# The two branch gates as 2x2 by 2x2 block products of seven, three formed inside the recurrence and four after it

## The chip, the cores and the metric

The kernel runs on one core of one Trainium2 chip. The metric is the device time of one launch in microseconds (us); a comparison takes the median of several runs. All arithmetic that counts is float32, so a matrix product is made of three matmuls: each operand x is split into a rounded high part h (fp32r) and a low part l = x - h, and hh + hl + lh is accumulated in PSUM.

## The reference, cut to what matters

```python
xn = rmsnorm(x, norm1_g)                   # 1024 tokens x 1024 channels
u  = xn @ w_in                             # q,k,v | f,i,q,g of HGRN2 | gate_sb | gate_hg
o_sb = stick_breaking_attention(q_sb, k_sb, v_sb)
o_hg = rmsnorm(hgrn2(silu(q_hg), k_hg, i_hg, log_f)) * silu(g_hg)
g_a = sigmoid(gate_sb + bg[:1024]);  g_b = sigmoid(gate_hg + bg[1024:])
merged = g_a * (o_sb @ w_o_sb) + g_b * (o_hg @ w_o_hg)
h = x + merged @ w_out
h = h + square(relu(rmsnorm(h) @ w_ff1)) @ w_ff2
out = rmsnorm(h) * final_g
```

The change concerns the two gates: `gate_sb` and `gate_hg` are each xn (1024 x 1024) times 1024 columns of `w_in`, and the two products with `w_o_sb` and `w_o_hg` that they scale.

## The kernel before, in words

Channels lie on partitions, tokens on the free axis, in two halves of 512 tokens (`halves`). `xn` is kept as eight pairs of tiles (`Acts`: high and low part, for each half of the tokens and each 256 channels). A product of one block of 128 output channels with one half of the tokens is `proj_half` (L471): eight k-tiles of 128 channels, three matmuls of 128x512 each (`three`, L466), so 24 matmuls into one PSUM bank.

The stages are: norm and transposes, attention, recurrence of HGRN2, gates and output projections, `w_out` with the second norm, MLP up (`UpPair`) and MLP down. The MLP products are already made as 2x2 block products of seven.

The engines' order is written by the program. Work that fills TensorE is put in a `Stream` (L413): a list of jobs, each with weight units that are loaded and split one or two jobs ahead (`prefetch`), and a generator that yields every six matmuls. The recurrence of the four heads runs as "main" work: `hg_levels` makes per head one diagonal product (`sd`) and seven levels (`sl`), where VectorE scales k and q between two levels, and `hg_tail` carries the state across chunks (`pk`, `pkv`, `pho`, `pot`). Between two pieces of main work the driver at L1476 takes FILL steps (2.8 to 4) from the stream; `upto` says how far the stream may go in each head. A scheduling layer then orders each engine's queue by these priorities, allots the buffers (40 full slots of 128x1024, 10 half slots, two each of `raw`, `whi`, `wlo`, eight PSUM banks) and puts in the waits. Each engine and the DMA queue of SP work through their queue in order.

The gates are jobs of that stream: for each branch (`which`) and each of eight column blocks (`cb`) one `proj_jobs` with `gate_epilogue` (L958, ScalarE's sigmoid with bias), 48 matmuls of 128x512. After every two blocks comes `out_job` (L968): the output projection of that branch (12 matmuls for each block and half), multiplied by the gate on VectorE. Branch 0 runs as fill of the recurrence (`pjg00` to `pjg07`, `py00` to `py07`), branch 1 after it, then `merged_split` makes the split tiles `ms` that `w_out` reads.

In `hg_tail` the loops write one 128-column piece of a PSUM bank and have it read (VectorE at L885 and L887 for `pkv`, ScalarE's square at L908 for `pho`) before the next piece is written.

Of the kernel before, what the change touches and what calls it, by code (L numbers as in the profile page):

```python
# [9 lines left out]
F32 = mybir.dt.float32  # L10
# [9 lines left out]
P = 128  # L20
# [8 lines left out]
NHG = 4  # L29
# [10 lines left out]
def kernel(  # L40
# [79 lines left out]
    def matmul(*a, **k):  # L120
        return pe(nc.tensor.matmul(*a, **k))  # L121
# [740 lines left out]
    def hg_tail(h):  # L862
# [32 lines left out]
        yield  # L895
        ons = []
        for half in range(2):
            open_block("main")
            po = bank(f"pho{h}_{half}")
            ssq = small.tile([P, 4], F32, tag="ssq4", name=f"hss{h}_{half}")  # L900
            sq = small.tile([P, P], F32, tag="sq", name=f"hsq{h}_{half}", bufs=1)
            for j in range(4):
                c = 4 * half + j
                cs, js = slice(c * P, (c + 1) * P), slice(j * P, (j + 1) * P)
                matmul(po[:, js], sc[:, cs], v[:, cs], start=True, stop=c == 0)
                if c:
# [40 lines left out]
            return h[:, s], l[:, s]  # L947

    a_sb, a_hg = Split("asb"), Split("ahg")
    mg, gate = {}, {}  # L950
    mgs = Acts("ms")

    def merged_split(half, kp):
        hi, lo = mgs.make(half, kp)
        for j, cs in halves():
            hi_lo(hi[:, cs], lo[:, cs], mg[2 * kp + j][:, half * 512 : (half + 1) * 512])

    def gate_epilogue(which, cb):  # L958
        def ep(ps, half):
            if half == 0:  # L960
                gate[which, cb] = slot(f"g{which}{cb}")
            b = prm[:, BG + which * KT + cb : BG + which * KT + cb + 1]
            dst = gate[which, cb][:, half * 512 : (half + 1) * 512]
            nc.scalar.activation(dst, ps, AF.Sigmoid, bias=b)  # L964

        return ep

    def out_job(which, cp):  # L968
        mat = (W_OSB, W_OHG)[which]
        src = mat[:, cp * 256 : (cp + 1) * 256].rearrange("(k p) c -> p k c", p=P)  # L970
        unit = Unit(f"wo{which}{cp}", [[(0, 256, src)]])
        acts = (a_sb, a_hg)[which]

        def body():
            if which == 1 and cp == 3:
                for kp in range(3):
                    merged_split(1, kp)
            for half, cs in halves():
                for j in range(2):
                    cb = 2 * cp + j  # L980
                    ps = bank(f"py{which}{cb}_{half}")
                    yield from proj_half(
                        ps, unit.hl[0], acts.mov, 4, half, lambda k: k * 256 + j * P
                    )
                    g = gate[which, cb][:, cs]
                    if which == 0:
                        if half == 0:
                            mg[cb] = slot(f"mg{cb}")
                        mul(mg[cb][:, cs], ps, g)
                    else:  # L990
                        mul(g, ps, g)
                        nc.vector.tensor_tensor(
                            out=mg[cb][:, cs], in0=mg[cb][:, cs], in1=g, op=ALU.add
                        )
                if which == 1 and (half == 0 or cp == 3):
                    merged_split(half, cp)
                    if cp == 3:
                        st.prefetch()

        return st.add([unit], body)  # L1000

    j_out = {}
    for which in range(2):
        for cp in range(4):
            for cb in (2 * cp, 2 * cp + 1):
                c0 = (C_GA, C_GB)[which] + cb * P
                u = cols_unit(f"wg{which}{cb}", [(W_IN, c0, P)])
                proj_jobs([(f"pjg{which}{cb}", u, gate_epilogue(which, cb))], xn)
            j_out[which, cp] = out_job(which, cp)


    hres = []
    scratch = ctx.enter_context(
        tc.tile_pool(name="scratch", bufs=1, space=bass.MemoryType.DRAM)
    )

    def dram(name, shape):
        return scratch.tile(shape, F32, tag=name, name=name)

    hn = Quads()  # L1020
    hsrc, hd = {}, {}
# [13 lines left out]
    def wout_job(n):  # L1035
        cs = slice(n * 512, (n + 1) * 512)
        units = [
            Unit(
                f"wout{n}{i}",
                [[(0, 512, W_OUT[i * 256 : (i + 1) * 256, cs].rearrange("(k p) c -> p k c", p=P))]],  # L1040
                wide=True,
            )
            for i in range(4)
        ]

        def body():
            for tb in range(NT):
                if n == 0:
                    hres.append(slot(f"h{tb}"))
                    load(hres[tb], X[tb * P : (tb + 1) * P, :])  # L1050
                    if tb in AHEAD_AT:
                        st.prefetch()
# [10 lines left out]
        return st.add(units, body)  # L1063

    AHEAD_AT = (2, 4, 6)
    for n in range(2):
# [4 lines left out]
    NPAIR, NCH = FF // 256, FF // 512  # L1071
    ad = [dram(f"ad{c}", [P, 7, 2, 512]) for c in range(NCH)]

    def half(name, dt=F32):
        return hpool.tile([P, 512], dt, tag="h", name=name)
# [5 lines left out]
    def add(out, a, b):  # L1081
        nc.vector.tensor_tensor(out=out, in0=a, in1=b, op=ALU.add)

    def sub(out, a, b):
        nc.vector.tensor_tensor(out=out, in0=a, in1=b, op=ALU.subtract)

    class UpPair:
        def __init__(self, j):
# [384 lines left out]
    st.finish(j_hg[0])  # L1473


    FILL = (2.8, 2.8, 2.8, 3, 4)  # L1476
    owed = 0.0
    turns = 0
    for h in range(NHG + 1):
        lev = hg_levels(h) if h < NHG else iter(())  # L1480
        tail = hg_tail(h - 1) if h > 0 else iter(())
        upto = (j_hg[2], j_hg[3], j_hg[3] + 2, j_out[0, 1], j_out[0, 3])[h]
        going = True
        while going:
            going = False
            if h == NHG - 2:
                p = len(a_sb.t)
                turns += 1
                if turns > 3 and p < 4:
                    a_sb.put(p, osb[p])  # L1490
# [15 lines left out]
    st.finish(j_wout - 2)  # L1506
    st.advance(7, j_wout - 1)
    first[0].load()
    first[0].split()
    first[0].sums()  # L1510
    st.finish(j_wout - 1)
    first[1].load()
    g2b[0] = slot("g2b")
    load(g2b[0], norm2_g[0].partition_broadcast(P))
    for tb in range(NT):
        st.advance(1, j_wout)
        if tb == 1:
            first[1].split()
            first[1].sums()
# [11 lines left out]
            pass  # L1531
        if tb == 6:
            hn.sums(1, 1)
    st.finish(j_wout)
    pairs[2].load()
    first[1].w1(0, 256)
    first[0].w2(0, 256)
# [65 lines left out]
```

## Time and profile before

| | |
|---|---|
| median of 3 runs | 1518.85 us (1517.78 to 1519.51) |
| the profiled execution | 1516.4 us, of which the span of instructions is 1514.6 us |
| granted TensorE clock | 0.999 |
| busy: PE, VectorE (DVE), ScalarE (ACT), GpSimd (POOL) | 1483.2, 962.1, 616.2, 69.1 us |
| DMA | 172.21 MB, mean 114 GB/s |

Stages in the span: norm and attention to about 329 us, recurrence with its fill to about 632 us, the rest of the gates and output projections to 795 us, `w_out` and second norm to about 900 us, then the MLP. PE counts matmuls, PEld weight loads. A matmul's end is modelled, so the distance between starts tells more than its duration. "L121" is the helper `matmul`; the tiles tell the products apart: `pjg` gates and HGRN2's g, `py` output projections, `sd` and `sl` the recurrence's levels, `pk`, `pkv`, `pho`, `pot` its tail. In the chain that ended last each row has its start, its length, the engine, the tile and the number of instructions.

### The profile page before, as it was taken

Reading aid. Unit: us, or ns where it says so; the run is one execution under the profiler, and the core shown is the slowest. Engines: PE = TensorE matmul, PEld = TensorE weight load, DVE = VectorE, ACT = ScalarE, POOL = GpSimd, SP = SyncE. Lnnn points to the kernel's source line nnn. Section 1 sums busy time; section 2 is a strip of 40 time slices with the busy share of each in tenths; the row PEclk is TensorE's granted clock in tenths of the full one; section 3 lists DMA queues with packets and bytes.
Section 4 is the critical chain, followed back from the end, with each engine's and each line's share of the span. In section 5 each row is a group of like instructions: output and inputs, shape, how many; then the busy total and the mean of one; then the engine's idle time right before and its main releaser. Section 6 shows DMA issues by size and latency. Waiting matters only on the chain.

```text
span 1514.6 us, 19739 instructions
## 1 busy us (share of the span) xinstructions
PE 1483.2 (98%) x7677; PEld 1258.7 (83%) x7677; DVE 962.1 (64%) x1379; ACT 616.2 (41%) x1091; POOL 69.1 (5%) x242
## 2 busy tenths in 40 slices
PE   7999999999999999999999999999999999999997
PEld 6888988988898888888888888888888878888886
DVE  5689798786535554232344479766666857757765
ACT  6566566541312211222232275444444434443433
POOL 2011010000000000000000000000000000000020
PEclk9999999999999999999999999999999999999999
DMA  7123012001101011111115232344444996654744
GB/s 202 29 56 77 8 53 67 15 15 43 57 1 42 29 38 33 42 56 42 56 56 195 111 107 96 127 153 152 153 153 153 341 374 250 222 202 172 260 141 170
DMA packets 125716, 172.21 MB, mean 114 GB/s; under 512 B 22924, under 2 KB 76216, under 8 KB 125624
## 3 DMA queue, kind: packets, MB, share of 16 engines
q1 hardware_dynamic: 124088, 166.77, 32.2%
q0 software_dynamic: 1536, 4.20, 1.2%
q8 instruction: 60, 0.98, 0.3%
q14 instruction: 32, 0.26, 0.0%
HBM read 129.00 MB, written 37.75 MB: 110 GB/s over the span
## 4 chain that ended last, share of the span: by engine, by line
PE 77%; DVE 5%; issue 5%; ACT 2%; DMA 2%; POOL 1%; SPq 0%; POOLq 0%; DVEq 0%; ACTq 0%
PE pm L121 15%; PE pjg L121 14%; PE pX L121 8%; PE py L121 6%; PE pY L121 5%; PE pW L121 5%; PE pw L121 4%; PE sl L121 3%; PE pjf L121 3%; PE pji L121 3%; PE pjq L121 2%; PE po L121 2%; PE pjv L121 1%; DVE rm L646 1%; PE z L121 1%
## 5 line engine op out<-in xcount | busy, mean ns | idle before, releaser
L134 ACT CAST whid<-w 128x1024 fp32r<-128x1024 f32 x31 | 32.7, 1055 | 166.7 <-PE pm L121 114.9
L646 DVE TENSOR_TENSOR_SCAN rm<-rm,bits 128x895 f32<-128x895 f32 (+5 forms) x64 | 86.1, 1349 | 18.8 <-ACT rm L627 17.1
L121 PE MATMUL pm<-whid,sl 128*128 128x512 f32 x248 | 96.6, 389 | 0.7 <-DVE sl L137 0.7
L121 PE MATMUL pm<-whid,sh 128*128 128x512 f32 x248 | 96.6, 390 | 0.6 <-ACT sh L134 0.6
L121 PE MATMUL pm<-wlod,sh 128*128 128x512 f32 x248 | 96.5, 389 | 0.0
L121 PE MATMUL pm<-th,sl 128*128 128x512 f32 x200 | 77.9, 390 | 0.4 <-DVE sl L137 0.4
L121 PE MATMUL pm<-tl,sh 128*128 128x512 f32 x200 | 77.8, 389 | 0.0
L121 PE MATMUL pm<-th,sh 128*128 128x512 f32 x200 | 77.8, 389 | 0.0
L137 DVE TENSOR_TENSOR sl<-sa,sh 128x1024 fp32r<-128x1024 f32 x56 | 68.3, 1220 | 2.0 <-ACT sh L134 2.0
L137 DVE TENSOR_TENSOR wlod<-w,whid 128x1024 fp32r<-128x1024 f32 x31 | 37.9, 1224 | 39.9 <-ACT whid L134 39.6
L134 ACT CAST wTh<-pw 128x128 fp32r<-128x128 f32 (+3 forms) x96 | 44.0, 484 | 45.9 <-PE pw L124 42.8
L134 ACT CAST sh<-sa 128x1024 fp32r<-128x1024 f32 x56 | 57.9, 1049 | 3.4 <-DMA sa<-ad 3.2
L121 PEld LDWEIGHTS pm<-whid,sl 128*128 128x128 f32 x248 | 46.5, 188 | 10.8 <-DVE sl L137 1.2
L121 PEld LDWEIGHTS pm<-whid,sh 128*128 128x128 f32 x248 | 46.6, 188 | 10.7 <-ACT sh L134 1.0
L137 DVE TENSOR_TENSOR wTl<-pw,wTh 128x512 fp32r<-128x512 f32 (+3 forms) x96 | 50.5, 547 | 7.6 <-ACT wTh L134 4.5
L121 PEld LDWEIGHTS pm<-wlod,sh 128*128 128x128 f32 x248 | 46.5, 188 | 9.6
L121 PEld LDWEIGHTS sl<-q,k 128*128 128x128 f32 (+1 forms) x448 | 50.2, 184 | 2.9 <-issue 1.1
L144 DVE TENSOR_TENSOR bt<-bt,rm 128x895 f32<-128x895 f32 (+5 forms) x64 | 48.2, 755 | 5.0 <-ACT bt L630 0.3
L121 PE MATMUL sl<-q,k 128*128 128x128 f32 (+1 forms) x448 | 51.3, 268 | 0.0
L964 ACT ACTIVATE g<-pjg,prm 128x512 f32<-128x512 f32 x32 | 21.9, 686 | 71.7 <-PE pjg L121 71.7
L121 PE MATMUL pX<-sqh,t1l 128*128 128x512 f32 x128 | 49.9, 390 | 0.5 <-DVE t1l L137 0.5
L627 ACT ACTIVATE rm<-z 128x511 f32<-128x511 f32 (+6 forms) x96 | 47.3, 500 | 7.6 <-DVE bt L144 4.5
(798 smaller groups left out, 4398.6 us busy)
## 6 DMA issues: line engine op xcount, KB each, us to landing
w<-in_w_ff_dram SPq DMA_DIRECT2D x72, 512.0 KB, 4.5
sa<-ad SPq DMA_DIRECT2D x56, 512.0 KB, 6.9
ad<-a SPq DMA_DIRECT2D x32, 256.0 KB, 3.8
ad<-s SPq DMA_DIRECT2D x16, 512.0 KB, 3.3
x<-in_x_dram SPq DMA_DIRECT2D x8, 512.0 KB, 4.5
h<-in_x_dram SPq DMA_DIRECT2D x8, 512.0 KB, 8.0
hd<-h SPq DMA_DIRECT2D x8, 512.0 KB, 2.7
ad<-p SPq DMA_DIRECT2D x16, 256.0 KB, 4.5
```

The source lines that it names most:

```text
L121: return pe(nc.tensor.matmul(*a, **k))
L134: after(nc.scalar.copy(dst, src), hold[0])
L137: return nc.vector.tensor_tensor(out=dst, in0=src, in1=hi.bitcast(F32), op=ALU.subtract)
L144: nc.vector.tensor_tensor(out=out, in0=a, in1=b, op=ALU.mult)
L627: nc.scalar.activation(rm[:, s0 + c0 - 1 : s0 + m - 1], z[:, c0:m], AF.Sigmoid, scale=-0.125)
L646: nc.vector.tensor_tensor_scan(out=rr, data0=rr, data1=bits[:, 1024 - nk : 1023][:, ::-1], initial=0.0, op0=ALU.mult, op1=ALU.max,)
L964: nc.scalar.activation(dst, ps, AF.Sigmoid, bias=b)
```

## The change

Both gates are taken together as one block product. The token halves are rows 1 and 2 of a 2x2 matrix A (A11, A12, A21, A22: half of the tokens by half of the channels of xn), and the columns of branch a and branch b are the columns of a 2x2 matrix B. For each of the eight column blocks seven products (of 12 matmuls of 128x512) replace eight.

- Three on the plain xn: A11 B11, then A22 times a difference of weights, then A12 B21 (`raw_job`, 36 matmuls). They run as fill of heads 2 and 3. Their results go to DRAM (`pd`, and the finished gate of branch a for the first half, `gd`).
- The output projection of branch a (`sb_job`) comes behind them as fill; it reads `gd` back and writes its products to DRAM (`yd`). Beside it `sum_forms` makes four sums of A's blocks: eight DMAs of 512 KB on POOL's queue that add the high tile onto the low tile in SBUF, then adds, subtractions and splits on VectorE and ScalarE.
- The other four products and the output projection of branch b run after the recurrence (`gates`): per block X6, Y5, X7, the late half's projection, Y3, the early half's projection, 72 matmuls. The next block's weights are loaded, differenced and split meanwhile (`GatePair.split`), `pd` and `yd` are loaded back, and three quarters of the late half's merged rows go through DRAM (`md`).
- In `hg_tail` the pieces of `pkv` and of `pho` are all written before the first is read.
- FILL is 3 throughout, `upto` follows the new jobs, and `w_out` has a stream of its own that splits ahead from its first job.

```diff
-        def __init__(self):
+        def __init__(self, eager=False):
...
-            if self.pos > 0:
+            if self.pos > 0 or self.eager:
                 self.prefetch()
...
                 matmul(pkv[:, js], ktk[:, cs], v[:, cs], start=True, stop=True)
+            for j in range(4 - half):
+                c = 4 * half + j
+                cs, js = slice(c * P, (c + 1) * P), slice(j * P, (j + 1) * P)
                 dst = Ss[:, (c + 1) * P : (c + 2) * P]
...
                     matmul(po[:, js], qh[:, cs], Ss[:, cs], start=False, stop=True)
+            for j in range(4):
+                js = slice(j * P, (j + 1) * P)
                 nc.scalar.activation(sq, po[:, js], AF.Square, accum_out=ssq[:, j : j + 1])
...
+    class RawUnit(Unit):
...
+            hi_lo(h, l, ra)
+            sub(rb, ra, rb)
+            sub(rb[:, 512:], rb[:, 512:], rb[:, 0:512])
+            self.hl = [(h, l)]
...
+    def raw_job(cb):
...
+        def body():
+            p1, p14, g1 = (half(f"{n}_{cb}") for n in ("p1", "p14", "g1"))
+            ps, p4 = bank(f"pga{cb}"), bank(f"pgq{cb}")
+            yield from steps_of(ps, 0, 0, 0, 0, True)
+            nc.scalar.copy(p1, ps)
+            nc.sync.dma_start(pd[cb][:, 0, :], p1)
+            for v in raw_units[cb : cb + 2]:
+                v.split_t()
+            yield from steps_of(p4, 1, 0, 1, 4, True)
+            add(p14, p1, p4)
+            nc.sync.dma_start(pd[cb][:, 1, :], p14)
+            yield from steps_of(ps, 0, 4, 0, 4, False)
+            nc.scalar.activation(g1, ps, AF.Sigmoid, bias=gate_bias(0, cb))
+            nc.sync.dma_start(gd[cb], g1)
+            if cb >= 4:
+                a_sb.put(cb - 4, osb[cb - 4])
...
+    def sum_forms():
...
+        def whole(i, j, kp):
+            h, l = (t.bitcast(F32) for t in xn.t[i, 2 * j + kp])
+            nc.gpsimd.dma_start(l, h, accum_op=ALU.add)
+            raw[i, j, kp] = l
...
+        for i, j in ((1, 0), (1, 1), (0, 0), (0, 1)):
+            for kp in range(2):
+                whole(i, j, kp)
+        yield from range(4)
...
+            add(s1[kp], raw[1, 0, kp], raw[1, 1, kp])
+            sub(s2[kp], s1[kp], raw[0, 0, kp])
+            split(6, kp, s2[kp])
...
+    class GatePair:
...
+        def x7(self):
+            self.product(7, self.X, False)
+            p1, p14 = self.p[:, 0:512], self.p[:, 512:1024]
+            add(p1, p1, self.X)
+            add(p1, p1, self.Y)
+            add(p14, p14, self.X)
+            self.gate(p1, 1)
+            self.gate(p14, 0)
...
+    def gates():
+        for cb in range(KT):
+            v = gp[cb]
+            n = gp[cb + 1] if cb + 1 < KT else None
+            v.x6()
+            v.y5()
+            if n:
+                n.split()
+                n.load_sums()
+                if cb + 2 < KT:
+                    gp[cb + 2].load()
+            else:
+                wout_units[0][0].split()
+            v.x7()
+            v.late_half()
+            v.y3()
+            v.early_half()
...
-    FILL = (2.8, 2.8, 2.8, 3, 4)
+    FILL = (3, 3, 3, 3, 3)
...
-        upto = (j_hg[2], j_hg[3], j_hg[3] + 2, j_out[0, 1], j_out[0, 3])[h]
+        upto = (j_hg[2], j_hg[3], j_raw[5], j_sb[1], j_sb[3])[h]
...
-    st.finish(j_out[0, 3])
-    for h in range(NHG):
-        a_hg.put(h, ohg[h])
-    st.finish(j_out[1, 3])
+        if h > 1:
+            a_hg.put(h - 2, ohg[h - 2])
+    a_hg.put(NHG - 1, ohg[NHG - 1])
+    st.finish(j_sb[3])
+    gates()
```

More of the change, by code (lines that the diff above doesn't have):

```diff
@@ L949 @@
     a_sb, a_hg = Split("asb"), Split("ahg")
-    mg, gate = {}, {}
     mgs = Acts("ms")
[L953 to L1012, printed above, removed]
     scratch = ctx.enter_context(
@@ L1018, in dram, with half, add, sub @@
         return scratch.tile(shape, F32, tag=name, name=name)
+    def half(name, dt=F32):
+        return hpool.tile([P, 512], dt, tag="h", name=name)
+    def add(out, a, b):
+        nc.vector.tensor_tensor(out=out, in0=a, in1=b, op=ALU.add)
+    def sub(out, a, b):
+        nc.vector.tensor_tensor(out=out, in0=a, in1=b, op=ALU.subtract)
+    pd = [dram(f"pd{cb}", [P, 2, 512]) for cb in range(KT)]
+    gd = [dram(f"gd{cb}", [P, 512]) for cb in range(KT)]
+    yd = [dram(f"yd{cb}", [P, 2, 512]) for cb in range(KT)]
@@ new lines, with gate_bias, gate_cols, __init__ @@
+    md = [dram(f"md{kp}", [P, 2, 512]) for kp in range(KT // 2)]
+    def gate_bias(which, cb):
+        return prm[:, BG + which * KT + cb : BG + which * KT + cb + 1]
+    def gate_cols(which, cb):
+        c0 = (C_GA, C_GB)[which] + cb * P
+        return slice(c0, c0 + P)
+    class RawUnit(Unit):
+        def __init__(self, cb):
+            dmas = [
+                [(0, P, W_IN[:, gate_cols(w, cb)].rearrange("(k p) c -> p k c", p=P))]
+                for w in range(2)
+            ]
+            super().__init__(f"wga{cb}", dmas)
+        def split(self):
+            if self.hl is not None:
+                return
+            self.load()
+            ra, rb = self.raw
+            h, l = (
+                wpool.tile([P, 1024], F32R, tag=t, name=f"{self.name}{t}") for t in ("whi", "wlo")
+            )
+            hi_lo(h, l, ra)
+            sub(rb, ra, rb)
+            sub(rb[:, 512:], rb[:, 512:], rb[:, 0:512])
+            self.hl = [(h, l)]
+        def split_t(self):
+            if len(self.hl) == 1:
+                t = slot(f"{self.name}t", F32R)
+                self.hl.append((t[:, 0:512], t[:, 512:]))
+                hi_lo(*self.hl[1], self.raw[1][:, 512:])
@@ new lines, with steps_of @@
+    raw_units = [RawUnit(cb) for cb in range(KT)]
+    def raw_job(cb):
+        u = raw_units[cb]
+        def steps_of(ps, wt, w0, half_, k0, start):
+            wh, wl = u.hl[wt]
+            for k in range(4):
+                c = (w0 + k) * P
+                xh, xl = xn.mov(k0 + k, half_)
+                three(
+                    ps, wh[:, c : c + P], wl[:, c : c + P], xh, xl, start and k == 0, k == 3, True
+                )
+                if k % 2 == 1:
+                    yield
+        def body():
[14 more added lines that the diff above has]
+                a_sb.put(cb - 4, osb[cb - 4])
+        return st.add([u], body)
@@ new lines, with sb_job, body @@
+    side = []
+    def sb_job(cp):
+        src = W_OSB[:, cp * 256 : (cp + 1) * 256].rearrange("(k p) c -> p k c", p=P)
+        unit = Unit(f"wo0{cp}", [[(0, 256, src)]])
+        def body():
+            if cp == 0:
+                side.append(sum_forms())
+            for j in range(2):
+                cb = 2 * cp + j
+                g1 = half(f"g1r{cb}")
+                load(g1, gd[cb])
+                for i, cs in halves():
+                    ps = bank(f"pys{cb}_{i}")
+                    for _ in proj_half(
+                        ps, unit.hl[0], a_sb.mov, 4, i, lambda k: k * 256 + j * P
+                    ):
+                        next(side[0], None)
+                        yield
+                    if i == 0:
+                        mul(g1, ps, g1)
+                        y = g1
+                    else:
+                        y = half(f"ys{cb}")
+                        nc.scalar.copy(y, ps)
+                    nc.sync.dma_start(yd[cb][:, i, :], y)
+        return st.add([unit], body)
@@ new lines, in late_merged @@
+    def late_merged(kp):
+        r = slot(f"mr{kp}")
+        load(r.rearrange("p (k t) -> p k t", k=2), md[kp])
+        hi_lo(*mgs.make(1, kp), r)
+    gp = [GatePair(cb) for cb in range(KT)]
+    def gates():
[9 more added lines that the diff above has]
+                    gp[cb + 2].load()
+            else:
+                wout_units[0][0].split()
[3 more added lines that the diff above has]
+            v.early_half()
@@ L1020 @@
+    hres = []
+    st2 = Stream(eager=True)
+    wout_units = []
     hn = Quads()
@@ L1044, in wout_job @@
         ]
+        wout_units.append(units)
         def body():
@@ L1048, in body @@
                 if n == 0:
+                    if tb < 3:
+                        late_merged(tb)
                     hres.append(slot(f"h{tb}"))
@@ L1061, in body @@
                 yield
-        return st.add(units, body)
+        return st2.add(units, body)
     AHEAD_AT = (2, 4, 6)
@@ L1079, in relu_square @@
         nc.scalar.activation(dst, dst, AF.Square)
[L1081 to L1085, printed above, removed]
     class UpPair:
@@ L1485 @@
             going = False
[L1486 to L1490, printed above, removed]
             for g in (lev, tail):
@@ L1510 @@
     first[0].sums()
-    st.finish(j_wout - 1)
+    st2.finish(j_wout - 1)
     first[1].load()
@@ L1533 @@
             hn.sums(1, 1)
-    st.finish(j_wout)
+    st2.finish(j_wout)
     pairs[2].load()
```

136 lines of the change are left out of this document (129 added, 7 removed).

## The prediction

> **What bounds the kernel now.** I read the page's engine shares first, then the chain of work that ended last, then busy time by stage, and last the rows that price the new work.
>
> ```profile
> span 1514.6 us, 19739 instructions
> PE 1483.2 (98%) x7677; PEld 1258.7 (83%) x7677; DVE 962.1 (64%) x1379; ACT 616.2 (41%) x1091; POOL 69.1 (5%) x242
> ...
> PE 77%; DVE 5%; issue 5%; ACT 2%; DMA 2%; POOL 1%; SPq 0%; POOLq 0%; DVEq 0%; ACTq 0%
> ```
>
> TensorE (PE) is busy 98% of the span and makes 77% of the chain. A mean over stages can hide one with another limit, so the stages from the recurrence to `w_out`:
>
> ```profile
> core 0: us, PE busy (x) PEld busy (x) DVE busy (x) ACT busy (x) POOL busy (x), PEclk, DMA share, GB/s
> 329.00:373.00 44.00, 44.00 (x264) 38.37 (x263) 31.69 (x83) 6.93 (x12) 0.00 (x0) 1.00 0.08 25
> 373.00:451.00 78.00, 77.77 (x526) 69.67 (x525) 37.73 (x83) 17.32 (x49) 2.45 (x4) 1.00 0.12 35
> 451.00:520.00 69.00, 69.00 (x398) 58.56 (x397) 42.73 (x88) 19.18 (x39) 2.40 (x4) 1.00 0.11 34
> 520.00:588.00 68.00, 68.00 (x385) 57.59 (x384) 34.27 (x74) 11.84 (x28) 2.40 (x4) 1.00 0.12 37
> 588.00:632.00 44.00, 44.00 (x232) 35.96 (x232) 13.92 (x26) 10.00 (x27) 2.40 (x4) 1.00 0.12 36
> 632.00:795.30 163.30, 163.30 (x722) 135.24 (x721) 56.22 (x70) 42.13 (x56) 0.00 (x0) 1.00 0.17 52
> ```
>
> The first four rows are heads 0 to 3 of the recurrence, the fifth its tail with fill, the sixth the remaining gates and projections. TensorE is busy throughout at full clock. VectorE (DVE) has 34.3 of 68 us in head 3 and 56 of 163 after the recurrence, and DMA is at 8 to 17%. So TensorE bounds every stage that the change touches: a matmul less is its price less, so long as nothing new starves TensorE.
>
> **The matmuls.** Before, the gates take 16 block products of 48 matmuls, 768 in all. After, each of eight blocks has 36 in the recurrence and 48 behind it, 672 in all. The projections (384), the levels and the tails keep their counts. The chain prices a matmul:
>
> ```profile
> 598.15 0.44 PE pkv L121 x4
> ...
> 632.09 21.76 PE pjg L121 x96
> 653.85 10.88 PE py L121 x48
> ...
> 795.29 65.45 PE pw L121 x288
> ```
>
> 21.76 us for 96 gate matmuls is 226.7 ns each, and the other two rows say the same. Exactly 96 go: **21.8 us less**.
>
> The Trainium skill, "TensorE: Matmul & The Clock Gate", section "Back-to-back issue gap", gives about 131 ns for a sustained matmul of 512 columns. By it the 96 would be an estimated 12.6 us and the forecast some 9 us higher; the rows above disagree with it for these fp32r operands and leave that no chance.
>
> Where the 96 go matters. FILL 3 puts about as many matmuls between two levels as before: by the order of TensorE's queue the stretch from head 1's first product to head 3's last level holds 564 of 512 columns before and 570 after. The saving stands behind the last level: from there to the first product of the stage after the recurrence, 198 matmuls are left; before, 300 stood there up to the first gate of branch b. So the levels aren't asked to run faster.
>
> **The tail loops.** Today a piece of `pho` waits until ScalarE has squared the one before it in the same bank:
>
> ```profile
> 605.29 0.22 PE pho L121 x2
> ...
> 606.67 0.55 PE pho L121 x4
> ...
> 607.92 0.53 PE pho L121 x4
> ...
> 615.46 3.43 PE pjg L121 x15
> ```
>
> Four records of `pkv` take 0.44 us without such a wait, those of `pho` mostly 0.53 to 0.56. From 605.29 to 615.46 stand 30 `pho` records and 27 fill matmuls: 30 x 0.11 + 27 x 0.2267 = 9.4 of 10.2 us, so some 0.7 us are waits. For four heads that is 2.8. With all pieces written first they go; ScalarE starts later by the length of a bank, 0.8 us, with fill beside it. I take **2.5 less** (bounds: 0, and 4.4 where `pkv` saves as well).
>
> **VectorE's added work.** Durations and distances:
>
> ```profile
> 573.88 0.42 DVE L144 TENSOR_TENSOR k<-k,pp 128x256 f32<-128x256 f32 x1 [4.27 <-PE sl L121]
> 574.22 0.42 DVE L144 TENSOR_TENSOR q<-q,pp 128x256 f32<-128x256 f32 x1
> ...
> 578.62 1.22 DVE L137 TENSOR_TENSOR wg04l<-wg04r,wg04h 128x1024 fp32r<-128x1024 f32 x1
> ...
> 587.94 0.69 DVE L144 TENSOR_TENSOR mg<-py,g 128x512 f32<-128x512 f32 x1 [1.56 <-PE py L121]
> 588.54 0.43 DVE L144 TENSOR_TENSOR k<-k,pp 128x256 f32<-128x256 f32 x1
> ```
>
> A 512-wide instruction lasts 0.69 us and the next starts after 0.60; a 1024-wide one lasts 1.22. In head 3 the raw jobs and splits put 14 of each on VectorE, 14 x 0.60 + 14 x 1.13 = 24 us (1.13 is the 1.22 less the same 0.09), where today seven of 512 and four of 1024 make 9. That lifts 34.3 to some 50 us of 66. In these levels VectorE sits idle before it until `sl` is done (4.27 us in the first row), and its share of a level, k and q scaled, is done about 2 us after `sl`, with 5 us or more of fill still to come; so I cost it at nothing where no load is late.
>
> After the recurrence one block is 72 matmuls, 16.3 us, and VectorE has 15 of 512 and two of 1024, 15 x 0.60 + 2 x 1.13 = 11.3 us, 69%. Two accumulations need care. X7 writes into X's bank again, so the add that reads X6 must be done; Y5 (2.7 us) covers it. Y3 writes into Y's bank, and the three adds after X7 come first: 0.60 + 0.60 + 0.69 = 1.9 us against the late projection's 12 matmuls, 2.7 us. Slack 0.8 us. The MLP up pass has the same shape:
>
> ```profile
> 900.00:925.00 25.00, 24.16 (x112) 19.35 (x112) 22.16 (x26) 17.99 (x23) 0.00 (x0) 1.00 0.18 64
> ...
> 1000.00:1025.00 25.00, 25.00 (x112) 20.69 (x111) 18.47 (x25) 12.25 (x19) 0.00 (x0) 1.00 0.44 150
> ```
>
> With VectorE at 74% TensorE loses nothing; at 89% it loses 0.8 of 25 us. So the steady blocks cost nothing, and I put **2 more** for the crowded places (head 3's raw loads, the first block, whose split follows the last sums).
>
> **The transfers.** `pd`, `gd`, `yd` and `md` write about 13 MB and read them back, spread over some 250 us; the DMA share there is 0.1 to 0.2. Prices:
>
> ```profile
> q0 software_dynamic: 1536, 4.20, 1.2%
> ...
> hb<-hd SPq DMA_DIRECT2D x8, 512.0 KB, 9.7
> ...
> QH<-QH POOLq DMA_DIRECT2D x16, 128.0 KB, 2.3
> ...
> wg04r<-in_w_in_dram SPq DMA_DIRECT2D x1, 512.0 KB, 3.7
> ```
>
> A gate weight lands 3.7 us after its issue, and a block's weights are issued a block ahead. SP's queue is passed by many new instructions: each store waits there for the engine that makes its tile, and the loads behind it wait too. In the order of SP's queue the loads of a block's weights stand behind the `md` store of the block before, done at about 14 of its 16.3 us, and wait for buffers that VectorE frees about 1 us into the next. They are needed some 5 us after that, against 3.7.
>
> The eight accumulating DMAs of 512 KB have no like in the trace. The first two may go early, two more when the last raw job has read its first channels, two when its middle product is done. VectorE's first sum needs the fifth of them, and behind that sum in VectorE's queue stands the copy of `fc`, for which ScalarE's copies of `pk` wait, and for these TensorE's `pkv` of head 3:
>
> ```profile
> L137 DVE TENSOR_TENSOR ahgl<-g,ahgh 128x1024 fp32r<-128x1024 f32 x4 | 4.8, 1219 | 0.0
> ...
> L865 DVE COPY fc<-pp 128x8 f32<-128x8 f32 x4 | 0.7, 171 | 0.1
> ...
> L874 ACT COPY pp<-pk 128x512 f32<-128x512 f32 x4 | 2.3, 584 | 12.4 <-PE pk L124 12.4
> L874 ACT COPY pp<-pk 128x384 f32<-128x384 f32 x4 | 1.9, 484 | 0.0
> ```
>
> TensorE has 42 matmuls, the last level (1.1) and `pk` (0.8) meanwhile: 11.4 us. The chain behind the landing takes 1.2 + 0.2 + 0.6 + 0.5 = 2.5. So landing within 8.9 us is free. Two others went onto the queue about 4.4 us earlier, so with b us of all engines for each DMA the third lands 3b - 3.9 after its release, and TensorE waits 3b - 12.8. The software queue's 1.2% of 1514.6 us for 4.20 MB makes b = 2.3 us for 512 KB; an addition reads two operands, so I take twice that, 4.5: a wait of 0.7, and as much again for the pieces of `pho` behind later sums, **1.5 more**. Bounds: nothing, and b = 9.7, the slowest 512 KB row: 16 us.
>
> The Trainium skill's "DMA: Bandwidth & Descriptors", section "Anatomy of one DMA — SWDGE (gpsimd) path", fits 2.0 us plus bytes at 436 GB/s, which the 2.3 us of the 128 KB row bears out; "Collectives: The Full Stack", section "The bandwidth ceiling: the fold count and why AG ≠ RS ≠ AR", says that an add needs two source reads and halves the rate. By both one such DMA is an estimated 4.4 us, and no row here shows an addition.
>
> **The sum.** -21.8 - 2.5 + 2.0 + 1.5 = -20.8 us against the profiled execution's own 1516.4 us (span 1514.6 and 1.8 around it): 1495.6. The median of the runs shown, 1518.85, lies 2.45 above that execution, so I forecast **1498** for the median.
>
> **Rivals.** First, the next block's weights land late. In every second block their three subtractions stand ahead of X7's adds on VectorE; with a landing over about 5.8 us the slack at Y3 is gone, and with the 9.7 of the slow row four blocks lose 3.9 us each: 1514 at worst, about 1506 midway. For it: stores and loads share SP's queue. Against: 3.7 us and a DMA share under 0.2. Chance 0.14. Second, the additions are slower than two reads: b between 5 and 11 gives 1500 to 1518. Chance 0.14, since nothing in the trace prices them. Third, slower than before, by the same place: from b = 11.8 us on, the wait of 3b - 12.8 eats all 22 us of gain; at b = 13 it is 26 us, 1522, and at twice the slow row (19.4) 45 us, 1541. Chance 0.09. That the matmuls don't go is no rival: the counts are in the program.
>
> **How the numbers follow.** The forecast has 0.63, from 1492 (no waits, tail loops at 4.4) to 1503. The first two rivals reach to 1513 for most of their weight, so 1492 to 1513 leaves out about 2 in 10. About 0.2%, 3 us, is what a measurement of this kernel can tell from no change. Faster than 1515.8: 0.87; within: 0.04; slower: 0.09.
>
> **What the new profile would show.** Right: the stretch from the last `sl` of head 3 to the first `gX` takes about 53 us, eight blocks of 16.3 us follow, TensorE is at 100% in both, the landing of `xnl` is under 9 us. Wrong: idle time of TensorE before `pkv` of head 3 put down to ScalarE or VectorE (second and third rival), or before Y3's matmuls put down to VectorE behind a DMA of `wg` (first rival); or blocks longer than 17 us.

## The result, and the profile after

The kernel after takes 1502.51 us (median of 4 runs, 1501.21 to 1502.69), the kernel before 1519.18 us in the same comparison (4 runs, 1517.78 to 1521.96): a ratio of 0.9886, with a 95% interval of 0.9869 to 0.9903. That is 16.7 us less, where 20.8 were forecast; the time lies inside the range and 4.5 us above the forecast.

The page of the kernel after (engine shares, the share of the chain that ended last, and the issue row of the new transfers: KB each and median us to landing):

```profile
span 1500.4 us, 19980 instructions
...
PE 1462.7 (97%) x7581; PEld 1245.7 (83%) x7581; DVE 1051.7 (70%) x1500; ACT 644.1 (43%) x1132; POOL 78.0 (5%) x250
...
q0 software_dynamic: 2688, 8.39, 2.8%
...
PE 68%; DVE 9%; issue 6%; DMA 6%; ACT 2%; POOL 1%; SPq 0%; POOLq 0%; DVEq 0%; ACTq 0%
...
xnl<-xnh POOLq DMA_DIRECT2D x8, 512.0 KB, 8.8
```

TensorE has 96 matmuls fewer and is still busy 97% of the span, but its part of the chain fell from 77 to 68%, and VectorE and DMA have 9 and 6% where they had 5 and 2. Something now ends later than TensorE. Busy time by stage (heads 0 to 3, the tail with its fill, the gates behind the recurrence) says where:

```profile
core 0: us, PE busy (x) PEld busy (x) DVE busy (x) ACT busy (x) POOL busy (x), PEclk, DMA share, GB/s
330.84:374.70 43.86, 43.86 (x263) 38.22 (x261) 31.88 (x83) 6.81 (x11) 0.00 (x0) 1.00 0.08 25
374.70:450.91 76.21, 76.21 (x525) 69.99 (x524) 37.70 (x83) 17.17 (x49) 2.45 (x4) 1.00 0.12 35
450.91:524.38 73.47, 71.77 (x411) 61.44 (x409) 46.77 (x90) 19.95 (x42) 4.20 (x6) 1.00 0.33 86
524.38:592.45 68.07, 66.93 (x391) 57.88 (x390) 54.31 (x103) 23.11 (x45) 7.72 (x9) 1.00 0.54 159
592.45:648.97 56.52, 54.04 (x261) 45.22 (x260) 39.71 (x52) 24.03 (x43) 5.63 (x6) 0.97 0.68 198
648.97:781.40 132.43, 130.90 (x578) 108.04 (x577) 94.01 (x133) 42.61 (x58) 0.00 (x0) 1.00 0.50 152
```

Before, TensorE was busy through these stages nearly without a break. Now it is idle for 1.7 us in head 2, 1.1 in head 3, 2.5 in the tail and 1.5 in the gates, while the DMA share rose from 0.1 to 0.3 to 0.7. The list of waits, for TensorE from 450 to 660 us (total, times, longest), names the places:

```profile
PE pho L121 <- DVE k L889: 2.3, 1, 2.3
PE pga L121 <- ACT p L1037: 1.7, 2, 1.1
PE gX L121 <- DVE gu L968: 1.5, 1, 1.5
PE sl L121 <- DVE q L144: 1.2, 2, 0.6
PE pkv L121 <- ACT pp L875: 0.2, 1, 0.2
```

The chain of that stretch, followed back from TensorE's late starts, tells what stood behind each:

```profile
494.91 8.01 DMA wga1r<-in_w_in_dram
...
507.99 5.27 DMA wga2r<-in_w_in_dram
...
578.97 0.49 ACT p L1037
...
579.50 3.03 PE pga L121 x12
...
591.46 13.31 DMA g1r<-gd
...
604.86 0.13 DVE g1r L144
...
605.47 1.22 DVE gsl L137
606.68 1.15 DVE gs L968
607.85 1.23 DVE gs L971
609.08 0.21 DVE k L889
...
609.34 2.35 PE pho L121 x10
...
646.36 3.00 DMA wg1r<-in_w_in_dram
...
655.46 0.60 DVE gu L968
...
656.11 3.04 PE gX L121 x12
```

Read it from a PE row upwards. At 609.34 `pho` starts late because VectorE copied a piece of the state (`k`, L889) at 609.08. That copy stood in VectorE's queue behind the multiplication by a gate read back from DRAM (`g1r`), whose transfer took 13.31 us for 256 KB, and behind 3.6 us of work on the sums (`gsl`, `gs`) between the two. At 656.11 X7 starts late because VectorE read X6 (`gu`) at 655.46, behind its work on the second block's weights, which landed at 649.4, and two multiplications by gates read back. At 579.50 a raw job's third product starts late behind ScalarE's copy of the first, and that stood behind splits which followed a weight load.

From the second block on the gates run as forecast (the same chain, further on): (765.23 - 667.31) / 6 = 16.3 us for each block.

```profile
667.31 2.72 PE gX L121 x12
...
683.63 2.72 PE gX L121 x12
...
765.23 2.72 PE gX L121 x12
```

**A ruler for what follows.** In the profiled executions the time before the recurrence goes from 329.0 to 330.9 us and the MLP's down pass from 315.0 to 320.0. That is more than several of the effects in question, though the program there is the same (save that the three `dram` kernels below add transfers to attention). So I measure the stretch from the recurrence's first product (`sd`) to the second norm's first transpose (`hnt`), which holds the whole change. Its ends are the first start in these rows, of before (first fence) and of after:

```profile
L121 PE MATMUL sd<-q,k x64: 270/275/275, 329.0 to 521.7; 128*128 128x128 f32 x64
L124 PE MATMUL hnt<-ident,hn x64: 270/272/329, 866.0 to 895.4; 128*128 128x128 f32 x64
```

```profile
L121 PE MATMUL sd<-q,k x64: 270/275/275, 330.8 to 526.0; 128*128 128x128 f32 x64
L124 PE MATMUL hnt<-ident,hn x64: 270/273/329, 852.2 to 881.6; 128*128 128x128 f32 x64
```

Before: 537.0 us. After: 521.4 us, 15.6 less; by the forecast's terms it should have been 516.2.

### The profile page after: what moved, and what is told of

The parts are those of the page before. It is cut to its first block, busy times and chain, and to the rows that moved or that the text cites. A ratio compares the mean times of both kernels' runs of the same rounds, so it can differ in the third digit from the quotient of the medians.

```text
span 1500.4 us, 19980 instructions
## 1 busy us (share of the span) xinstructions
PE 1462.7 (97%) x7581; PEld 1245.7 (83%) x7581; DVE 1051.7 (70%) x1500; ACT 644.1 (43%) x1132; POOL 78.0 (5%) x250
## 4 chain that ended last, share of the span: by engine, by line
PE 68%; DVE 9%; issue 6%; DMA 6%; ACT 2%; POOL 1%; SPq 0%; POOLq 0%; DVEq 0%; ACTq 0%
PE pm L121 15%; PE pX L121 8%; PE pY L121 5%; PE pW L121 5%; PE pw L121 4%; PE pyh L121 3%; PE pji L121 3%; PE pjf L121 3%; PE gX L121 3%; PE gY L121 3%; PE pjg L121 2%; PE pjq L121 2%; PE sl L121 2%; PE po L121 2%; PE pjv L121 1%
## 5 line engine op out<-in xcount | busy, mean ns | idle before, releaser
L137 DVE TENSOR_TENSOR sl<-sa,sh 128x1024 fp32r<-128x1024 f32 x56 | 68.3, 1219 | 3.3 <-ACT sh L134 3.3
L968 DVE TENSOR_TENSOR w<-w,w 128x1024 f32<-128x1024 f32 x24 | 29.3, 1222 | 29.9 <-DMA w<-in_w_ff_dram 29.8
```

What stands on the lines that cost most here:

```text
L137: return nc.vector.tensor_tensor(out=dst, in0=src, in1=hi.bitcast(F32), op=ALU.subtract)
```

## The experiments

Theory: the terms for the matmuls and the tail loops hold, and about 10 us are lost again, because the accumulating transfers take the DMA engines from the weights and read backs beside them. Rival: the loss is the load of VectorE and ScalarE in the crowded places, whatever the transfers do. All stretches by the ruler above; the kernel before ran beside each group of kernels (medians of 1518.60 to 1519.49), and a ratio is to its own group's; "head 2" is from its `sd` to head 3's, "head 3" from there to the last `sl`, "tail" from there to the first `gX`, "block 1" from there to the second block's.

| kernel | median us | ratio to before, 95% interval | stretch | head 2 | head 3 | tail | block 1 |
|---|---|---|---|---|---|---|---|
| before | 1519.18 | | 537.0 | 69.1 | 68.8 | | |
| m_less96 | 1496.48 | 0.9852 (0.9839 to 0.9865) | 515.6 | 69.1 | 68.7 | | |
| tails_only | 1513.70 | 0.9963 (0.9950 to 0.9975) | 532.8 | 68.3 | 68.0 | | |
| after | 1502.51 | 0.9886 (0.9869 to 0.9903) | 521.4 | 73.5 | 68.1 | 56.5 | 18.2 |
| plain_copies | 1495.36 | 0.9849 (0.9833 to 0.9866) | 513.1 | 71.0 | 67.2 | 52.0 | 18.0 |
| no_additions | 1496.51 | 0.9859 (0.9839 to 0.9879) | 512.7 | 71.0 | 66.6 | 51.9 | 18.0 |
| gate_early | 1498.85 | 0.9868 (0.9855 to 0.9882) | 518.4 | 73.4 | 67.6 | 54.0 | 18.1 |
| copy_first | 1501.94 | 0.9888 (0.9874 to 0.9902) | 519.6 | 72.5 | 66.6 | 57.9 | 17.6 |
| read_first | 1503.06 | 0.9899 (0.9885 to 0.9913) | 520.9 | 74.6 | 68.1 | 55.7 | 17.4 |
| split_early | 1499.86 | 0.9875 (0.9857 to 0.9893) | 519.1 | 74.3 | 66.7 | 56.3 | 16.6 |
| all_three | 1497.98 | 0.9866 (0.9847 to 0.9884) | 515.3 | 72.5 | 66.6 | 53.1 | 18.0 |
| dram_sums | 1497.57 | 0.9854 (0.9840 to 0.9867) | 515.8 | 72.1 | 68.2 | 52.0 | 18.6 |
| dram_all | 1495.12 | 0.9845 (0.9830 to 0.9860) | 512.8 | 71.1 | 66.6 | 52.0 | 18.1 |
| dram_split | 1493.80 | 0.9835 (0.9819 to 0.9851) | 511.1 | 71.0 | 66.6 | 52.0 | 16.5 |

Head 2 runs the same program in after, read_first and split_early and takes 73.5, 74.6 and 74.3 us: where transfers set the pace, about 1 us goes with the execution. A stretch is that of one traced execution. By the medians alone, only plain_copies and the three `dram` kernels are clear of the kernel after (their intervals don't overlap its own); the smaller steps between kernels rest on the stretches and on the waits listed.

**m_less96** (the matmuls alone, on the kernel before):

```diff
+                nk = 4 if which == 1 and cb >= 4 else KT
-                proj_jobs([(f"pjg{which}{cb}", u, gate_epilogue(which, cb))], xn)
+                proj_jobs([(f"pjg{which}{cb}", u, gate_epilogue(which, cb))], xn, nk)
...
```

> The kernel before, with four gates of branch b (column blocks 4 to 7) summed over half of the channels only: exactly 96 matmuls of 128x512 fewer, nothing added. Theory (a matmul of a TensorE-bound stage is worth its 226.7 ns): 21.8 us less than the kernel before. Rival (VectorE, ScalarE or the weight loads take over where matmuls go): 15 us less or fewer, with idle time of TensorE in the gates' stage.

Measured: the stretch is 21.4 us shorter (537.0 to 515.6), the median 22.5. The matmuls' term is right.

**tails_only** (on the kernel before; the loops for `pkv` and `pho` taken apart as in the change's diff, nothing else):

> The kernel before, with only the loops of the recurrence's tail taken apart (all pieces of a bank written before the first is read). Theory: 2.5 us less, as forecast, from the 30 matmuls of pho in each head. Rivals: 0, where VectorE's and ScalarE's later start gives the gain back; 4.4 less, where pkv saves as well.

Measured: 4.2 us (537.0 to 532.8), near the upper bound and not at the 2.5 taken. Head 1, whose fill holds head 0's tail, gains 1.8 (78.0 to 76.2 from its `sd` to head 2's), the three others 0.8 each. With the matmuls the two gains are 25.6 us, so without any loss the stretch would be 537.0 - 25.6 = 511.4. The kernel after stands 10.0 above that; the forecast gave 3.5 to losses.

**plain_copies** (the kernel after):

```diff
-            nc.gpsimd.dma_start(l, h, accum_op=ALU.add)
+            nc.gpsimd.dma_start(l, h)
```

> The kernel after, with each of the eight accumulating transfers made a plain copy of the high part over the low part (this leaves the low part out of the sums' operands); every engine's order is the same. Theory (an addition reads two operands, and six of them in a row fill the DMA engines from 584 to 608 us): a copy takes about half of an addition, 1.5 to 2 us against 3 of all engines' time and 4 to 5 us to land in place of 8.8, the read back of the gate lands in under 8 us in place of 13.3, and TensorE's wait of 2.3 us before pho goes: about 2 to 2.5 us less than the kernel after. Rival (the additions are no slower than copies; 512 KB from SBUF to SBUF is what fills the engines): landing stays at 8 us or more and the wait stays.

Measured: 8.3 us off the stretch, far more than expected: 2.5 in head 2, 0.9 in head 3, 4.6 in the tail. No engine's order changed, so VectorE and ScalarE have the same work in the same queues. A 1024-wide addition on VectorE lasts 1.22 us in both kernels during the burst. That decides against the rival for these places. TensorE's waits from 450 to 660 us in this kernel:

```profile
PE gX L121 <- DVE gu L968: 1.3, 1, 1.3
PE pga L121 <- ACT p L1037: 0.2, 1, 0.2
```

The DMA view of the burst shows why; first the kernel after from 584 to 606 us, then plain copies from 580 to 597 (queue: packets, MB, share of the 16 engines' time; issues with median us to landing):

```profile
q0 software_dynamic: 793, 2.92, 72.2%
q1 hardware_dynamic: 1373, 2.09, 27.0%
...
xnl<-xnh POOLq DMA_DIRECT2D x6, 512.0 KB, 10.9
```

```profile
q0 software_dynamic: 864, 3.15, 50.4%
q1 hardware_dynamic: 1597, 2.49, 41.1%
...
xnl<-xnh POOLq DMA_DIRECT2D x6, 512.0 KB, 5.3
```

In both windows the engines are nearly full (99 and 92%). An addition takes 0.722 x 22 us / (2.92 / 0.524) = 2.85 us of all engines, a copy 0.504 x 17 / 6 = 1.43. From the first issue of the six to the last landing the burst lasts 24.1 us (584.4 to 608.6) in place of 16.7 (580.2 to 596.9), and the read back `g1r` beside it takes 6.6 us in place of 13.3. The same holds for the two early additions in head 2. A weight load issued just behind them (`wga1r`) took 8.01 us in the chain above and 5.15 in this kernel's:

```profile
494.05 5.15 DMA wga1r<-in_w_in_dram
...
504.26 5.15 DMA wga2r<-in_w_in_dram
```

The next load then starts at 504.26 and not at 507.99 (head 2 itself begins at 450.0 and 450.9), 2.9 us sooner within the head, and the waits of `pga` and `sl` at 517 to 521 us are gone.

**no_additions** (the kernel after, the line above taken out):

> The kernel after without the eight accumulating transfers (the sums are made of the low parts alone, so this leaves the high parts out of four of the products); VectorE's first sums also move ahead, into head 3's last levels. It bounds what the additions and their lateness cost in all. Theory: the waits of 0.3 us before pkv and 2.3 us before pho go, and with sums finished earlier the 1.5 us in the first block of the gates too: 2.5 to 4.3 us less than the kernel after. Rival (the lost time is VectorE's load, not the transfers): within 1 us of the kernel after.

Measured: 8.7 us, twice what was expected, and about what plain copies give. TensorE keeps one wait, 1.4 us before X7 of block 1: earlier sums don't help there.

**gate_early** (the kernel after; the last raw job issues the first read back):

```diff
+            if cb == KT - 1:
+                early[0] = half("g1r0")
+                load(early[0], gd[0])
...
```

> The kernel after, with the first read back of a finished gate (g1r of block 0) issued one job earlier, ahead of the burst of additions. Theory: VectorE's 2.7 us wait for that transfer held up the copies of pkv's results, and through them TensorE before pho; the wait of 2.3 to 2.5 us before the first pho that reads the state goes, so about 2.3 us less than the kernel after (1500). Rival (VectorE is simply too full there with the sums): VectorE gains 2.7 us but the sums take them, and TensorE's wait stays at 1.5 us or more.

Measured: 3.0 us, 2.5 of them in the tail. The wait of 2.3 us before `pho` falls to 0.2 and 0.3 in two places, while the wait before `pkv` rises from 0.2 to 0.8. So the late read back was a link between the burst and TensorE, and 2.5 of the tail's 4.6 us went by way of it. The other 2.1 stay (54.04 us against 51.95 with plain copies): at most that much is the additions' own lateness, by the waits before `pkv` and `pho`, 1.3 us in the list.

**copy_first** (the kernel after):

```diff
-            nc.scalar.copy(p1, ps)
+            hold[0] = nc.scalar.copy(p1, ps)
...
                 v.split_t()
+            hold[0] = None
```

(`hold` puts ScalarE's splits behind the instruction that it names.)

> The kernel after, with ScalarE's copy of a raw job's first product put ahead of the splits of the next weights in its queue. Theory: the waits of 0.5 and 1.1 us (0.7 and 1.3 of distance) before the third product of raw jobs 1 and 7 came from this copy standing behind a split that waited for weights from DRAM; both go, about 2 us less than the kernel after. VectorE's splits come a little later, so the two waits of 0.55 and 0.62 us before sl of head 3's last level may stay. Rival (the splits made later are the next wait): the time comes back before the second product of the following raw job, within 1 us of the kernel after.

Measured: 1.7 us. The waits of `pga` and `sl` are gone, but the first raw job's own split now comes late (1.2 us before `pgq`), and the wait before `pho`, which this edit doesn't touch, grew to 4.0 us. Partly the theory, partly the rival.

**read_first** (the kernel after; the first of the second block's subtractions ordered behind the read of X6):

```diff
-            sub(r0[:, s0], r0[:, s1], r0[:, s0])
+            after(sub(r0[:, s0], r0[:, s1], r0[:, s0]), behind)
...
```

> The kernel after, with VectorE's read of the first block's X6 put ahead of its subtractions for the second block's weights. Theory: the 1.5 us before X7 of the first block came from that read standing behind subtractions that waited for weights and for ScalarE's split; it goes, and nothing else moves: 1.5 us less than the kernel after. Rival (the second block's weights are the limit): the split ends later by about 3 us, and TensorE waits before the second block's X6 or X7 instead.

Measured: block 1 takes 17.4 us in place of 18.2. The wait before X7 is gone, and 0.8 us before Y3 stands in its place: the rival, in part. The stretch is 0.5 us shorter and the median 0.6 longer, so no gain is shown for the kernel as a whole.

**split_early** (the kernel after; in `sum_forms`):

```diff
+        gp[0].split()
+        gp[1].load()
         for kp in range(2):
             s4 = slot(f"gs4{kp}")
...
-        gp[0].split()
-        gp[1].load()
```

> The kernel after, with the first block's weights split, and the second block's weights loaded, ahead of the last sums and not behind them. Theory (X7 of the first block waits since VectorE's read of X6 stands behind the second block's weights, which are late because they are loaded behind the last sums): their loads go out about 4 us earlier, the 1.5 us wait before X7 goes and nothing comes in its place: the first block takes 16.3 us against 18.2, 1.8 less than the kernel after. Rival (VectorE is simply full there): the first block stays above 17 us, with the wait before X7, Y3 or X6.

Measured: block 1 takes 16.6 us, 1.5 less, and neither X7, Y3 nor X6 waits. So VectorE is not too full: the second block's weights were late because their loads stood behind the last sums.

**all_three** (gate_early, copy_first and read_first together):

> The kernel after with the three rearrangements together: the gate's first read back issued a job earlier, ScalarE's copy ahead of the splits, VectorE's read of X6 ahead of the next weights. Theory (the three losses are separate): 2.3 + 2.0 + 1.5 = 5.8 us less than the kernel after, about 1496.5 us. Rival (they hand the same wait on): 2 us less or fewer.

Measured: 6.1 us off the stretch, 4.5 off the median. Waits of 1.2 us (`pgq`) and 1.4 us (Y3) remain.

**dram_sums** (the kernel after; the additions moved to where the DMA engines have room):

```diff
+    def keep_whole(q):
+        i, j, kp = q
+        h, l = (t.bitcast(F32) for t in xn.t[i, 2 * j + kp])
+        after(nc.gpsimd.dma_start(xd[q], h), last_q[0])
+        nc.gpsimd.dma_start(xd[q], l, accum_op=ALU.add)
...
-            nc.gpsimd.dma_start(l, h, accum_op=ALU.add)
+            nc.gpsimd.dma_start(l, xd[i, j, kp])
...
```

> The kernel after, with high plus low part of each of the eight pieces of xn put together in DRAM during attention (a plain store and an accumulating one each), and read back by plain loads where the additions stood. Theory (what the additions cost in heads 2 and 3 and the tail is the room they take on the DMA engines beside weights and read backs): the loads take a plain copy's time, so from the recurrence's first product to the second norm's transposes the kernel takes 513 us as with plain copies, against 521.4 after and 537.0 before, and the median falls by about 8 us to 1494. Rival: accumulating onto DRAM beside attention's own transfers delays attention, so its first 330 us grow by more than 3 us.

Measured: 515.8, 5.6 us less than after and 2.7 more than plain copies; the median is 1497.6, not 1494. Attention isn't delayed (the recurrence starts at 330.0 us). The tail is as short as with plain copies. What is left are waits of `pga` (1.2), `sl` (0.8) and X7 (1.9).

**dram_all** (with gate_early, read_first, and copy_first from the second raw job on):

> As the sums made in DRAM, with the three rearrangements on top (first read back of a gate a job earlier, ScalarE's copy ahead of the splits except in the first raw job, VectorE's read of X6 ahead of the next weights). Theory (with the additions gone only two waits are left, 0.4 us before the last raw job's third product and 1.5 us in the first block): 1 to 1.5 us less than with the sums in DRAM alone, the wait in the first block not fully gone since Y3 then waits. Rival: nothing, or some time lost in the first raw jobs, within 0.5 us either way.

Measured: 3.0 us less, twice what was expected, since dram_sums had kept more waits than plain copies. Only Y3 of block 1 waits, 1.5 us.

**dram_split** (as dram_all, with split_early in place of read_first):

> The sums made in DRAM, the first read back of a gate a job earlier, ScalarE's copy ahead of the splits except in the first raw job, and the first block's weights split ahead of the last sums. Theory: the waits that were left go together; from the recurrence's first product to the second norm's transposes 511.1 us against 512.8 with the rearrangement of VectorE's read and 521.4 in the kernel after, a median of about 1493.5. Rival (the sums end later and are late themselves): 512.5 us or more.

Measured: 511.1 us, as expected, and a median of 1493.80, the lowest of all. No wait of TensorE is listed from 450 to 660 us. Heads 2 and 3, the tail, and the gates:

```profile
450.97:521.97 71.00, 71.00 (x410) 61.52 (x409) 46.69 (x93) 20.06 (x42) 3.56 (x6) 1.00 0.29 86
521.97:588.60 66.63, 66.63 (x391) 57.94 (x390) 54.51 (x100) 23.24 (x45) 5.16 (x9) 1.00 0.57 180
588.60:640.55 51.95, 51.95 (x261) 43.78 (x260) 40.72 (x54) 23.94 (x43) 5.96 (x5) 1.00 0.64 214
640.55:771.40 130.85, 130.85 (x578) 108.18 (x577) 93.71 (x133) 43.44 (x59) 0.00 (x0) 1.00 0.48 147
```

TensorE is busy in all of every stage, at nearly the DMA share of the kernel after and with VectorE's busy time the same within 1 us. The stretch is 25.9 us shorter than before, and the two gains measured alone are 25.6: the account closes to 0.3 us.

## Why the prediction was right, and where it was off

- **The matmuls, 21.8 less.** Right: 21.4 alone.
- **The tail loops, 2.5 less.** The mechanism was right, the size was not: 4.2, near the bound of 4.4.
- **Two more for the crowded places** (head 3's raw loads, the first block). Heads 2 and 3 lost 73.5 - 71.0 and 68.1 - 66.6, 4.0 us in all against dram_split, block 1 another 1.7. Head 3 and the first block were named; head 2, which lost most, was not. The cause was wrong for the heads: I put it down to VectorE's load, but with plain copies 3.4 of the 4.0 went while that load stayed. In the first block it was the order that I named (a split behind the last sums), and not a full VectorE. The load itself came as forecast: 54.3 of 68 us in head 3 against some 50 of 66, and 71% behind the recurrence against 69%.
- **The additions, 1.5 more.** This is the step that failed: the term was mis-sized, since it had no price for what stands beside the additions. I priced them only where their own sums are awaited. There the landing came out as in my formula, and by luck: the third of the six (issued at 588.95, landed at 598.6) took 9.6 us, 0.7 more than the 8.9 that are free, and 3 x 4.5 - 3.9 is 9.6 too. But one addition takes 2.85 us of all engines and not 4.5, by which the formula gives 4.7; it has nothing for engines shared with other transfers. TensorE waited 0.2 us there. What I left out is that the additions hold the engines while other transfers are needed. The two early ones delayed the raw weights, 2.5 us in head 2 and 0.9 in head 3. The six in a row delayed `g1r`, 2.5 of the tail's 4.6 us; the other 2.1, at most, are the lateness that I had priced at 1.5. Plain copies take 8.3 us off, against 1.5 in my sum, or 3.5 with the crowded places.
- **The first rival** (the next block's weights late, X7's adds behind them) has a likeness in the first block alone, 1.5 us before X7. But there the weights were issued late, behind the sums, and landed 3.0 us after; the slow landing that the rival needs (over 5.8 us) didn't come. From the second block on the slack held.
- **The second and third rivals** had the additions slow by themselves. The numbers that they needed (5 us and more for each) didn't come; most of the damage came through the neighbours.
- **What the profile would show.** The blocks of 16.3 us came, except the first. The 53 us from the last `sl` to the first `gX` became 56.5, and are 52.0 where the burst is gone. TensorE at 100% failed by 2.5 us in the tail and 1.5 in the gates. The median landing was 8.8 us, under the 9 that I named; that sign said nothing of the transfers beside it.

In sum: 1.7 us more gain from the tails, 0.4 less from the matmuls, 6.5 more lost than allowed for, which is the 5.2 between 516.2 and 521.4. Of the 6.5, 1.7 are a halved TensorE clock behind the wait in the tail (last section), for which the sum had no term. That the median still fell within 1492 to 1503 owes something to luck: it lies 0.5 us below the upper end, with losses of 10.0 us in place of 3.5.

Left open: why one 256 KB read back on the other queue takes 13.3 us while that queue has 27% of the engines' time. And since I didn't run the kernel after with the old tail loops, their gain there is inferred from the closed account.

## What to carry to other kernels

Price a new transfer twice: by when its own reader needs it, and by the engine time that it takes from every load and read back issued in the same 20 us; a stage whose DMA share reads 0.1 before the change has no spare room once a burst fills it. An experiment that keeps every engine's order and makes the transfer cheaper (a copy for an addition) tells the two apart in one run. And in an in-order queue, look at what stands in front of a short instruction on the main path: three of the four longest waits here were for a copy or a read of 0.3 to 0.7 us that stood behind work for later.

## What the runs showed of the hardware

TensorE's clock halved after the wait before `pho`. The kernel after, in short windows around the end of that idle time at 609.34 us (the column behind the busy times is the mean granted clock of the window):

```profile
608.00:609.30 1.30, 0.00 (x0) 0.00 (x0) 1.28 (x2) 0.19 (x1) 0.00 (x0) 1.00 1.01 365
609.30:610.00 0.70, 0.66 (x4) 0.67 (x5) 0.65 (x2) 0.70 (x1) 0.00 (x0) 0.67 0.64 212
610.00:611.00 1.00, 1.00 (x6) 1.00 (x6) 0.85 (x2) 1.00 (x2) 0.00 (x0) 0.50 0.83 274
611.00:612.00 1.00, 1.00 (x6) 0.90 (x5) 1.00 (x3) 1.00 (x3) 0.00 (x0) 0.50 0.25 86
612.00:613.00 1.00, 1.00 (x4) 0.81 (x3) 1.00 (x3) 0.94 (x7) 0.00 (x0) 0.53 0.00 0
```

The trace's clock record has the half from 609.53 to 612.94 us. It lost about 0.33 x 0.7 + 0.5 + 0.5 + 0.47 = 1.7 us more, so this wait of 2.3 us cost 4. With it the tail's listed waits of 2.5 us come to 4.2 of the 4.6 that it lost. The same happened behind the same wait in split_early (2.3 us) and copy_first (4.0), but not in read_first, where TensorE was idle for 2.6 us up to 610.08:

```profile
607.20:609.70 2.50, 0.32 (x3) 0.13 (x2) 2.47 (x3) 0.00 (x0) 0.00 (x0) 1.00 1.00 335
609.70:610.70 1.00, 0.62 (x5) 0.62 (x6) 0.93 (x4) 0.84 (x1) 0.00 (x0) 1.00 0.79 254
```

So the length of the wait alone doesn't decide. In the clock records of all fourteen traces, changes lie whole multiples of 3.413 us apart. Counted on from a trace's first record, the idle 2.33 us of the kernel after fall inside one such period (606.12 to 609.53), while those of read_first are parted at 608.45 into 0.9 and 1.6. That would explain the difference; no run tests it, and no sharp limit follows: elsewhere a period with 1.6 us idle was followed by the half clock (gate_early, from 1203.2 us) and one with 1.7 was not (read_first, from 516.3 us). Behind the idle 1.5 us in the gates the clock stayed at 1.00. The Trainium skill, "TensorE: Matmul & The Clock Gate", section "HAM oscillation — how this bites in real kernels", warns of idle gaps over about 3.4 us; here 2.3 us were enough in two kernels and 2.6 us were not in a third, so the measurement differs from that rule.

An addition of 512 KB within SBUF takes 2.85 us of all DMA engines and a copy 1.43: twice as much. The two early ones, alone with one weight load, take 3.15 and 1.75 (57.2 and 31.8% of 11 us, halved). Twice is what the Trainium skill, "Collectives: The Full Stack", section "The bandwidth ceiling: the fold count and why AG ≠ RS ≠ AR", says of an add's two source reads. The trace agrees with the ratio; that the second read is its cause no run here shows.
